# A hybrid decoder layer on one core: the running sum of the state-space decays and its three-way split are issued behind the first pair of stick-breaking heads

## The chip, the cores and the metric

The kernel runs on one core of a Trainium2 chip. The metric is the device time of one execution in microseconds (us); the time given for a kernel is the median of its runs.

## The reference, cut to what matters

The layer takes 1024 tokens behind 16 learned meta tokens (1040 positions), width 1024. One normalised input feeds three groups of heads, whose outputs are joined: stick-breaking attention (8 heads of 64), a state-space mixer (16 heads) and a latent attention (8 heads). A gated feed-forward stage follows. The change concerns the first two groups. Of the mixer it concerns the step sizes `dt`, and `Acs`, the running sum of the decays `dA` within a block of 128 positions, which the mixer's scan uses much later.

```python
dt = jax.nn.softplus(dt_raw.astype(F32) + dt_bias.astype(F32)) * valid[None, :, None].astype(F32)
a = -jnp.exp(a_log.astype(F32))
...
dA = (dt * a).reshape(b, nc, BLOCK, G, J)
Acs = jnp.cumsum(dA, axis=2)
...
seg = Acs[:, :, :, None] - Acs[:, :, None, :]
Ldec = jnp.exp(jnp.where(tri[None, None, :, :, None, None], seg, -jnp.inf))
...
z = jnp.einsum('bqhd,bkhd->bhqk', qb.astype(F32), kf) * scale
log_1m = jnp.where(mask, jax.nn.log_sigmoid(-z), 0.0)
between = lax.cumsum(log_1m, axis=3, reverse=True) - log_1m
w = jnp.exp(jnp.where(mask, jax.nn.log_sigmoid(z) + between, -jnp.inf))
return jnp.einsum('bhqk,bkhd->bqhd', w, vf)
...
h = h + jnp.concatenate([o_sb, o_ssm, o_mla], axis=-1) @ w_out[i].astype(dt)
```

## The kernel before, in words

All products are made of float32 operands split into a high and a low part, so a dense product is three matmuls per slice (lines 142 to 144 in `dense_fm`: high by high, low by high, high by low), accumulated in one of the two PSUM buffers of the pool `dpsum` (tile `d_ps`). One dense group for a chunk of positions is 24 matmuls. A buffer comes free when ScalarE (ACT) and VectorE (DVE) have copied its result out (`evac`).

The stretch that matters begins at about 80 us. The input has been normalised, keys and queries of the first pair of heads are ready (pair 0), and the program text gives, in this order: the value loads of pair 0, `step_sizes`, and then for each of four pairs `sb_attend`, the key and query products of the next pair, the next pair's values, and three of the twelve convolution units (`conv_unit`).

- `sb_attend` (line 676): for each of two heads and for j = 0 to 3, two rows of scores (`sb_row`) and one weighted sum (`weighted_values`). A row i covers 144 + 128 i keys: scores on TensorE (lines 661 to 665, tile `sc_ps`), a sigmoid on ACT (line 667) and a running product on DVE (line 669, tile `cm`, four buffers). The weighted sum transposes the rows on TensorE (lines 307 to 319, tiles `ptm` and `ptg`, pool `tp` with two buffers), splits them on ACT (302, 309) and DVE (303, 310), multiplies by the values (292 to 296, 311, tile `pv`, one buffer) and copies out (332 on ACT, 334 on DVE).
- The key copies of a pair (`k_evac`) are lines 591 and 592 on ACT and 593 and 594 on DVE, and those of the queries 600 and 601. The key tiles come from a ring `K` of four buffers.
- `conv_unit` (line 471): for each of three chunks a dense group, then ACT scales it into a tile of the ring `cacc` (479), three multiply-adds on DVE read the PSUM buffer (486), ACT takes a sigmoid into a tile of the ring `csig` (490), POOL multiplies (491) and a DMA stores. `cacc` and `csig` have two buffers each (pool `fl`), handed out in the order of the program text.
- `step_sizes` (line 410): a dense group of 96 columns, nine transposes into a `tp` buffer (`dtt`, 422), ACT's Abs and Exp (433, 434), then a softplus series on DVE (437 to 449), whose last result is the tile `d1`. Then comes what the change moves, lines 450 to 469: one matmul with a triangle of ones (`acum`, 451), its copy to `AT` (452), nine transposes (`acst`, 460), three copies on ACT (462) into `acs`, and eighteen DVE instructions that split `acs` into three bfloat16 parts of `A3` (463 to 469). `acs` lies in `raws[2]` and `raws[3]`, two of the four buffers of the ring `K`; `a2` (466) is a tile of the ring `csig`.

The order on each engine is not the program text's: a scheduler takes the instructions in the text's order of priority and places each on its engine's queue when, by its own plan, the operands and buffers are there. On the chip each engine then works through its queue in that order.

Of the kernel before, what the change touches and what calls it, by code (L numbers as in the profile page):

```python
# [11 lines left out]
F32 = mybir.dt.float32  # L12
# [12 lines left out]
T = SEQ + META  # L25
# [33 lines left out]
def tile_hybrid_block(ctx: ExitStack, tc: tile.TileContext, a: dict):  # L59
# [64 lines left out]
    def load_w(src, cols=1024, wp=None, make=None):  # L124
        wp = wp or wa
        raw = wp.tile([128, 1024], F32, tag="wraw", bufs=1, name="wraw")
        sp.dma_start(raw[:, :cols], src)
        hi = make("whi") if make else wp.tile([128, 1024], F32R, tag="whi", name="whi")
        act.copy(hi[:, :cols], raw[:, :cols])  # L129
        lo = make("wlo") if make else wp.tile([128, 1024], F32R, tag="wlo", name="wlo")  # L130
        pool.tensor_tensor(lo[:, :cols], raw[:, :cols], f32(hi[:, :cols]), op=ALU.subtract)  # L131
        return hi, lo

    def dense_fm(dpool, w, nkt, m, mov, chunks, evac):
        hi, lo = w
        for c0, n in chunks:
            ps = dpool.tile([128, 512], F32, tag="d", name="d_ps")
            for kt in range(nkt):
                mh, ml = mov(kt, c0, n)
                wh = hi[:, kt * m : (kt + 1) * m]  # L140
                wl = lo[:, kt * m : (kt + 1) * m]
                pe.matmul(ps[:m, :n], wh, mh, start=(kt == 0), stop=False)  # L142
                pe.matmul(ps[:m, :n], wl, mh, start=False, stop=False)  # L143
                pe.matmul(ps[:m, :n], wh, ml, start=False, stop=(kt == nkt - 1))  # L144
            with tc.high_priority(offset=1000):
                evac(ps, c0, n)
# [44 lines left out]
    def fill_tile(tag, name):  # L191
        return fl.tile([128, 388 if tag == "craw" else 384], F32, tag=tag, name=name)
# [13 lines left out]
    raws = [sbq.tile([128, 1024], F32, tag=tag, name="raw") for tag in ("KS", "KS", "K", "K")]  # L206
# [203 lines left out]
    def step_sizes():  # L410
        NC = 9 * 16
        pt = tp.tile([128, 512], F32, tag="tp", name="dtt")

        def dt_evac(ps, c0, n):
            dtx = fill_tile("cacc", "dtx")
            act.activation(dtx[:16, :n], ps[0:16, :n], AF.Identity, bias=dtb)
            krt = fill_tile("csig", "krt")
            act.copy(krt[:96, :n], ps[:96, :n])
            act.dma_start(s_kr[:, c0 : c0 + n], krt[32:96, :n])
            for b, (t0, w) in enumerate(BLOCKS):  # L420
                if c0 <= t0 < c0 + n:
                    pe.transpose(pt[:w, b * 16 : b * 16 + 16], dtx[:16, t0 - c0 : t0 - c0 + w], ident[:16, :16])

        dense_fm(dpool, load_w(a["w_dt"], KT * 96), KT, 96, hn_mov, CH_ALL, dt_evac)

        dx = fill_tile("cacc", "dx")[:, :NC]
        d1 = fill_tile("craw", "d1")[:, :NC]
        d2 = fill_tile("csig", "d2")[:, :NC]
        dve.memset(dx[:, 0:16], 0.0)
        dve.tensor_copy(dx[:META, 0:16], pt[:META, 0:16])  # L430
        dve.tensor_copy(dx[:, 16:NC], pt[:, 16:NC])
        dtv = DT.rearrange("p b h -> p (b h)")
        act.activation(d1, dx, AF.Abs)
        act.activation(d1, d1, AF.Exp, scale=-1.0)
        act.activation(acol, acol, AF.Exp)

        dve.tensor_scalar(d2, d1, 2.0, None, ALU.add)
        dve.reciprocal(d2, d2)
        dve.tensor_tensor(d1, d1, d2, op=ALU.mult)
        dve.tensor_tensor(d2, d1, d1, op=ALU.mult)  # L440
        dve.tensor_scalar(dtv, d2, 1.0 / 17, None, ALU.mult)
        for k in (15, 13, 11, 9, 7, 5, 3):
            dve.scalar_tensor_tensor(dtv, dtv, 1.0 / k, d2, ALU.add, ALU.mult)
        dve.scalar_tensor_tensor(dtv, dtv, 1.0, d1, ALU.add, ALU.mult)
        dve.tensor_scalar(dtv, dtv, 2.0, None, ALU.mult)
        dve.scalar_tensor_tensor(dtv, dx, 0.0, dtv, ALU.max, ALU.add)
        dve.tensor_scalar(acol, acol, -1.0, None, ALU.mult)
        d13 = d1.rearrange("p (b h) -> p b h", h=16)
        dve.tensor_tensor(d13, DT, acol.unsqueeze(1).to_broadcast([128, 9, 16]), op=ALU.mult)
        pt = tp.tile([128, 512], F32, tag="tp", name="acum")  # L450
        pe.matmul(pt[:, :NC], tri, d1, start=True, stop=True)
        dve.tensor_copy(AT.rearrange("p b h -> p (b h)"), pt[:, :NC])

        pool.memset(A3, 0.0)
        for i, (t0, n) in enumerate(CH_ALL):
            acs = (raws[2][:16, 0:272], raws[2][:16, 512:896], raws[3][:16, 0:384])[i]
            pt = tp.tile([128, 512], F32, tag="tp", name="acst")
            for b in range(3 * i, 3 * i + 3):
                b0, w = BLOCKS[b]
                pe.transpose(pt[:16, b0 - t0 : b0 - t0 + w], AT[:w, b, :], ident[:w, :w])  # L460
            c = slice(t0, t0 + n)
            act.copy(acs[:, :n], pt[:16, :n])
            dve.tensor_copy(A3[0:16, c], acs[:, :n])
            dve.tensor_tensor(acs[:, :n], acs[:, :n], A3[0:16, c], op=ALU.subtract)
            dve.tensor_copy(A3[32:48, c], acs[:, :n])
            a2 = fl.tile([16, 384], BF16, tag="csig", name="a2")
            dve.tensor_copy(a2[:, :n], acs[:, :n])
            dve.tensor_tensor(acs[:, :n], acs[:, :n], a2[:, :n], op=ALU.subtract)
            dve.tensor_copy(A3[64:80, c], acs[:, :n])
# [165 lines left out]
    for i, (q0, qn) in enumerate(((0, 256), (256, 384), (640, 384))):  # L635
# [3 lines left out]
        c0, n = CH_ALL[i]  # L639
# [8 lines left out]
    with ctx_sb as st:  # L648
        sbb = st.enter_context(tc.tile_pool(name="sbb", bufs=2, side="right", reuse_waits="tile"))
        sc = st.enter_context(tc.tile_pool(name="sc1", bufs=3, space=PSUM, reuse_waits="tile"))  # L650
        pvp = st.enter_context(tc.tile_pool(name="pv1", bufs=1, space=PSUM, reuse_waits="tile"))

        def sb_row(Qh, Kh, KSh, i):
            n_all = META + 128 * (i + 1)
            cm = sbb.tile([128, T], F32, tag="cm", bufs=4, name="cm")
            qs = Qh[:, 128 * i : 128 * (i + 1)]
            chunks = key_chunks(i)
            for c0, n in chunks[::-1]:
                ps = sc.tile([128, 512], F32, tag="sc", name="sc_ps")
                last = c0 + n >= n_all  # L660
                pe.matmul(ps[:, :n], qs, Kh[:, c0 : c0 + n], start=True, stop=False)
                pe.matmul(ps[:, :n], qs, KSh[:, c0 : c0 + n], start=False, stop=not last)
                if last:
                    m0 = n_all - 128 - c0
                    pe.matmul(ps[:, m0 : m0 + 128], identr, sb_mask, start=False, stop=True)
                    n = n_all - c0
                act.activation(cm[:, c0 : c0 + n], ps[:, :n], AF.Sigmoid, scale=-0.125)  # L667
            rev = cm[:, 0:n_all][:, ::-1]
            dve.tensor_tensor_scan(rev, rev, zcol.to_broadcast([128, n_all]), 1.0, ALU.mult, ALU.add)  # L669
            return cm  # L670

        pms = meta_tiles(sbb)

        def sb_attend(p, proj, values):
            Q, K, KS = proj
            for h in range(2):
                for j in range(NQ // 2):
                    rows = [sb_row(Q[h], K[h], KS[h], 2 * j + e) for e in range(2)]  # L680
                    weighted_values(tp, pvp, sbb, j, rows, values[0], h, [x[p, 64 * h : 64 * (h + 1)] for x in (s_osbh, s_osbl)], pms[j % 2], values[1])

        values = load_value_steps(sbv, sbb, 0)
        step_sizes()
        convs = [8, 9, 10, 11, 0, 1, 2, 3, 4, 5, 6, 7]
        for p in range(4):
            sb_attend(p, proj, values)
            if p < 3:
                if p == 1:
                    sb_values(1, [load_w(a["w_sbv"][1, u]) for u in range(2)], range(9))  # L690
                proj, k_evac, q_evac = sb_project(p + 1)
                dense_fm(dpool, load_w(a["w_sbk"][p + 1]), KT, 128, hn_mov, CH_ALL, k_evac)
                dense_fm(dpool, load_w(a["w_sbq"][p + 1]), KT, 128, hn_real, CH_REAL, q_evac)
                values = load_value_steps(sbv, sbb, p + 1)
            for u in convs[3 * p : 3 * p + 3]:
                conv_unit(u)
# [1023 lines left out]
```

## Time and profile before

| | |
|---|---|
| median of 3 runs | 1817.64 us (1814.70 to 1820.21) |
| profiled execution | 1819.26 us |
| its span, first to last instruction | 1817.3 us |
| TensorE (PE) busy, matmuls | 1722.8 us, 95% |
| VectorE (DVE) busy | 1214.3 us, 67% |
| ScalarE (ACT) busy | 860.0 us, 47% |
| GpSimd (POOL) busy | 858.4 us, 47% |
| mean granted TensorE clock | 0.972 of full |

A busy share is a mean over the whole span; what bounds a stretch is read from the stretches. The granted clock has two levels, 2.4 GHz (1.00) and 1.2 GHz (0.50); a figure between them is a mean over a stretch that saw both, and time in which TensorE does nothing counts in the figure as well.

### The profile page before, as it was taken

To read this page: it belongs to the slowest core of one execution; us is meant where nothing else is said; L and a number is where in the kernel's file an instruction comes from. 1 tells how busy PE (TensorE), PEld (TensorE's weight loads), DVE (VectorE), ACT (ScalarE), POOL (GpSimd) and SP (SyncE) were. 2 spreads that over 40 slices of the span, in tenths; PEclk is the share of its full clock that TensorE was granted. 3 is DMA by queue.
4 is the path that set the end of the run, shared out by engine and by line. 5 is a ranking of instruction groups with operands and counts; after the bars stand their busy time and mean duration, and the time that the engine had idled before them with its cause. 6 is when DMAs were issued, how large, how long until landed. Compare 5 with 4: busy or idle time off the path is not lost.

```text
span 1817.3 us, 26447 instructions
## 1 busy us (share of the span) xinstructions
PE 1722.8 (95%) x9769; PEld 1506.0 (83%) x9769; DVE 1214.3 (67%) x1801; ACT 860.0 (47%) x1878; POOL 858.4 (47%) x597
## 2 busy tenths in 40 slices
PE   7969999999999999999999998999999999799997
PEld 7859998999987778998888876778888888677787
DVE  8686655777544673455576558967776667899854
ACT  7545564555566646775544424422232223334333
POOL 4433334343366557563321345634333234678783
PEclk9969999999998999999999998999999999899999
DMA  4211232222443546347221342232222233733102
GB/s 157 60 53 44 78 88 73 64 70 66 116 148 106 187 159 171 103 124 263 78 88 53 108 140 102 64 99 83 80 76 81 71 98 140 286 100 95 47 1 93
DMA packets 121012, 186.93 MB, mean 103 GB/s; under 512 B 21986, under 2 KB 81412, under 8 KB 120884
## 3 DMA queue, kind: packets, MB, share of 16 engines
q1 hardware_dynamic: 101488, 169.69, 29.6%
q10 hardware_dynamic: 19396, 15.56, 2.8%
q8 instruction: 77, 1.26, 0.3%
q14 instruction: 51, 0.42, 0.1%
HBM read 131.61 MB, written 53.60 MB: 102 GB/s over the span
## 4 chain that ended last, share of the span: by engine, by line
PE 68%; DVE 17%; ACT 4%; issue 3%; DMA 3%; POOL 3%; SPq 1%; ACTq 0%; DVEq 0%; POOLq 0%
PE d_ps L142 8%; PE d_ps L143 8%; PE d_ps L144 8%; PE b_ps L1295 7%; PE b_ps L1297 7%; PE b_ps L1296 7%; DVE raw L1081 2%; PE ptg L317 2%; PE b_ps L1498 1%; PE b_ps L1497 1%; PE ptg L319 1%; PE pv L295 1%; PE b_ps L1496 1%; PE pv L296 1%; DVE hF L1084 1%
## 5 line engine op out<-in xcount | busy, mean ns | idle before, releaser
L142 PE MATMUL d_ps<-hnh,whi 128*128 128x384 f32 (+6 forms) x744 | 247.3, 333 | 1.4 <-DVE go L534 0.7
L144 PE MATMUL d_ps<-hnl,whi 128*128 128x384 f32 (+6 forms) x744 | 246.7, 332 | 0.0
L143 PE MATMUL d_ps<-hnh,wlo 128*128 128x384 f32 (+6 forms) x744 | 245.6, 330 | 0.0
L131 POOL TENSOR_TENSOR wlo<-wraw,whi 128x1024 fp32r<-128x1024 f32 (+1 forms) x57 | 135.9, 2385 | 212.0 <-ACT whi L129 203.1
L1078 POOL TENSOR_TENSOR op<-raw,op 128x512 fp32r<-128x512 f32 x83 | 125.2, 1534 | 42.1 <-ACT op L1077 38.9
L142 PEld LDWEIGHTS d_ps<-hnh,whi 128*128 128x128 f32 (+1 forms) x744 | 140.4, 189 | 5.5 <-DVE go L534 1.3
L144 PEld LDWEIGHTS d_ps<-hnl,whi 128*128 128x128 f32 (+1 forms) x744 | 140.6, 189 | 3.3 <-issue 1.0
L143 PEld LDWEIGHTS d_ps<-hnh,wlo 128*128 128x128 f32 (+1 forms) x744 | 140.4, 189 | 2.3 <-issue 0.2
L1295 PE MATMUL b_ps<-T,wh 128*128 128x512 f32 x352 | 138.4, 393 | 0.9 <-DVE u L1084 0.9
L1296 PE MATMUL b_ps<-T,wl 128*128 128x512 f32 x352 | 138.1, 392 | 0.0
L1297 PE MATMUL b_ps<-T,wh 128*128 128x512 f32 x352 | 138.0, 392 | 0.0
L303 DVE TENSOR_TENSOR pl<-ptg,ph 128x512 fp32r<-128x512 f32 (+1 forms) x160 | 99.6, 628 | 46.3 <-ACT ph L302 44.7
L1078 POOL TENSOR_TENSOR wlo<-raw,whi 128x1024 fp32r<-128x1024 f32 (+1 forms) x22 | 52.7, 2395 | 152.9 <-ACT whi L1077 152.9
L669 DVE TENSOR_TENSOR_SCAN cm<-cm,zcol 128x144 f32<-128x144 f32 (+3 forms) x64 | 103.9, 1634 | 17.8 <-ACT cm L667 17.4
L1077 ACT CAST op<-raw 128x512 fp32r<-128x512 f32 x107 | 61.4, 618 | 96.7 <-PE d_ps L1498 49.4
L302 ACT CAST ph<-ptg 128x512 fp32r<-128x512 f32 (+1 forms) x160 | 85.3, 541 | 36.3 <-PE ptg L319 24.7
L1078 POOL TENSOR_TENSOR wl<-raw,wh 128x512 fp32r<-128x512 f32 x46 | 69.8, 1526 | 58.8 <-ACT wh L1077 58.0
L1084 DVE TENSOR_TENSOR hF<-hF,b_ps 128x512 f32<-128x512 f32 (+1 forms) x96 | 59.2, 635 | 46.4 <-PE b_ps L1562 23.9
L486 DVE SCALAR_TENSOR_TENSOR cacc<-d_ps,cw,cacc 128x384 f32<-128x384 f32 (+3 forms) x108 | 61.8, 572 | 38.2 <-ACT cacc L479 36.2
L1077 ACT CAST wh<-raw 128x512 fp32r<-128x512 f32 x88 | 52.9, 616 | 67.0 <-PE b_ps L1297 64.0
L129 ACT CAST whi<-wraw 128x1024 fp32r<-128x1024 f32 (+1 forms) x57 | 58.9, 1033 | 49.4 <-PE d_ps L144 23.4
L1496 PE MATMUL b_ps<-op 128*128 128x512 f32 x183 | 72.8, 401 | 9.9 <-DVE hF L1084 6.2
(452 smaller groups left out, 5352.8 us busy)
## 6 DMA issues: line engine op xcount, KB each, us to landing
raw<-in_w_gate_dram SPq DMA_DIRECT2D x22, 512.0 KB
raw<-in_w_up_dram SPq DMA_DIRECT2D x22, 512.0 KB, 4.1
s_hid<-gs SPq DMA_DIRECT2D x44, 256.0 KB, 2.4
raw<-in_w_down_dram SPq DMA_DIRECT2D x22, 512.0 KB, 5.2
raw<-s_hid SPq DMA_DIRECT2D x22, 512.0 KB, 4.3
wraw<-in_w_o_dram SPq DMA_DIRECT2D x16, 512.0 KB, 4.0
wraw<-in_w_xbc_dram SPq DMA_DIRECT2D x12, 512.0 KB, 3.8
s_xs<-csig SPq DMA_DIRECT2D x24, 192.0 KB, 2.6
```

Source lines behind the costliest of these rows:

```text
L131: pool.tensor_tensor(lo[:, :cols], raw[:, :cols], f32(hi[:, :cols]), op=ALU.subtract)
L142: pe.matmul(ps[:m, :n], wh, mh, start=(kt == 0), stop=False)
L143: pe.matmul(ps[:m, :n], wl, mh, start=False, stop=False)
L144: pe.matmul(ps[:m, :n], wh, ml, start=False, stop=(kt == nkt - 1))
L303: dve.tensor_tensor(pl[:, :n], pt[:, :n], f32(ph[:, :n]), op=ALU.subtract)
L669: dve.tensor_tensor_scan(rev, rev, zcol.to_broadcast([128, n_all]), 1.0, ALU.mult, ALU.add)
L1077: act.copy(hi, value)
L1078: eng.tensor_tensor(lo, value, f32(hi), op=ALU.subtract)
L1295: pe.matmul(banks[j], hi[:, ks], UH[u][k], start=start and k == 0, stop=False, skip_group_check=skip)
L1296: pe.matmul(banks[j], lo[:, ks], UH[u][k], start=False, stop=False, skip_group_check=skip)
L1297: pe.matmul(banks[j], hi[:, ks], UL[u][k], start=False, stop=stop and k == 3, skip_group_check=skip)
L1496: pe.matmul(banks[o], wh[:, os], hh, start=first, stop=False, skip_group_check=not start)
```

## The change

`step_sizes` ends with `d1` and returns it; what followed becomes `decay_sums`, which is called behind `sb_attend` of pair 0. `acs` no longer lies in the ring `K` but in a tile of the ring `cm` that the call takes. `a2` stays in the ring `csig`, `d1` in the ring `craw`. No instruction is added or taken away: one matmul, nine transposes, three ACT copies, nineteen DVE instructions and one memset (on POOL, at the start of the program in both). Nothing of it issues a DMA.

```diff
--- before.py
+++ after.py
@@ -447,13 +447,18 @@
         dve.tensor_scalar(acol, acol, -1.0, None, ALU.mult)
         d13 = d1.rearrange("p (b h) -> p b h", h=16)
         dve.tensor_tensor(d13, DT, acol.unsqueeze(1).to_broadcast([128, 9, 16]), op=ALU.mult)
+        return d1
+
+    def decay_sums(d1, space):
+
+        NC = 9 * 16
         pt = tp.tile([128, 512], F32, tag="tp", name="acum")
         pe.matmul(pt[:, :NC], tri, d1, start=True, stop=True)
         dve.tensor_copy(AT.rearrange("p b h -> p (b h)"), pt[:, :NC])
 
         pool.memset(A3, 0.0)
         for i, (t0, n) in enumerate(CH_ALL):
-            acs = (raws[2][:16, 0:272], raws[2][:16, 512:896], raws[3][:16, 0:384])[i]
+            acs = space[:16, t0 : t0 + n]
             pt = tp.tile([128, 512], F32, tag="tp", name="acst")
             for b in range(3 * i, 3 * i + 3):
                 b0, w = BLOCKS[b]
@@ -681,10 +686,12 @@
                     weighted_values(tp, pvp, sbb, j, rows, values[0], h, [x[p, 64 * h : 64 * (h + 1)] for x in (s_osbh, s_osbl)], pms[j % 2], values[1])
 
         values = load_value_steps(sbv, sbb, 0)
-        step_sizes()
+        steps = step_sizes()
         convs = [8, 9, 10, 11, 0, 1, 2, 3, 4, 5, 6, 7]
         for p in range(4):
             sb_attend(p, proj, values)
+            if p == 0:
+                decay_sums(steps, sbb.tile([128, T], F32, tag="cm", bufs=4, name="acs"))
             if p < 3:
                 if p == 1:
                     sb_values(1, [load_w(a["w_sbv"][1, u]) for u in range(2)], range(9))
```

The scheduler places almost everything between 92 and 272 us anew; the queues of all engines agree again from about TensorE's 1,575th matmul on (272 us), but for some neighbours that change places much later. Line numbers of the changed kernel are five higher from line 450 on, and seven from `sb_attend`'s calls on (661 is 666, 669 is 674, 486 is 491, 593 is 598).

TensorE where the second chunk of pair 1's keys ends (`d_ps<-hnh` and `hnl` are dense matmuls). Before:

```order
L144 MATMUL d_ps<-hnl_143,whi 128x384
L142 MATMUL d_ps<-hnh_136,whi 128x384
L143 MATMUL d_ps<-hnh_136,wlo 128x384
L144 MATMUL d_ps<-hnl_144,whi 128x384
L451 MATMUL acum<-d_1028,tri 128x144
L460 MATMUL acst<-identr,AT 16x16
L460 MATMUL acst<-identr,AT 16x128 x8
L307 MATMUL ptm<-identr,cm 16x128
L308 MATMUL ptm<-identr,cm 16x128
L317 MATMUL ptg<-identr,cm 128x128
```

and now:

```order
L142 MATMUL d_ps<-hnh_136,whi 128x384
L143 MATMUL d_ps<-hnh_136,wlo 128x384
L144 MATMUL d_ps<-hnl_144,whi 128x384
L666 MATMUL sc_ps<-K,Q 128x400
L667 MATMUL sc_ps<-KS,Q 128x400
L311 MATMUL pv<-pm,V 128x256
L307 MATMUL ptm<-identr,cm 16x128
L308 MATMUL ptm<-identr,cm 16x128
L295 MATMUL pv<-ph,V 128x128
L142 MATMUL d_ps<-hnh_129,whi 128x384
L143 MATMUL d_ps<-hnh_129,wlo 128x384
L144 MATMUL d_ps<-hnl_137,whi 128x384
```

The running sum no longer follows the second chunk; weighted sums of head 0 and the third chunk's matmuls (`hnh_129` again, lines 142 to 144) do.

VectorE at the end of the split. Before (`K` and `KS` are the keys' copies, `A` and `a` the bfloat16 parts):

```order
L468 TENSOR_TENSOR raw<-raw,a_1089 16x384
L469 CAST A_121<-raw 16x384
L334 TENSOR_TENSOR oT<-pv,half 64x2x128
L469 CAST A_121<-raw 16x384
L303 TENSOR_TENSOR pl<-ptg,ph 128x512
L669 SCALAR_TENSOR_TENSOR cm<-cm,zcol 128x912
L303 TENSOR_TENSOR pl<-ptg,ph 128x384
L593 TENSOR_TENSOR K<-d_ps,K 64x272
L594 TENSOR_TENSOR KS<-d_ps,K 64x272
```

and now, at the split's beginning:

```order
L303 TENSOR_TENSOR pl<-ptg,ph 128x384
L457 COPY AT<-acum 128x144
L334 TENSOR_TENSOR oT<-pv,half 64x2x128
L468 CAST A_121<-acs 16x272
L674 SCALAR_TENSOR_TENSOR cm<-cm,zcol 128x144
L469 TENSOR_TENSOR acs<-acs,A_121 16x272
L674 SCALAR_TENSOR_TENSOR cm<-cm,zcol 128x272
L674 SCALAR_TENSOR_TENSOR cm<-cm,zcol 128x400
L470 CAST A_121<-acs 16x272
L472 CAST a_1622<-acs 16x272
L468 CAST A_121<-acs 16x384 x2
L473 TENSOR_TENSOR acs<-acs,a_1622 16x272
```

The keys' copies of pair 1 no longer stand behind the split; the split stands behind the last weighted sum of pair 0 (`pl`), among the running products of pair 1 (`cm`).

TensorE in the second head of pair 0, now: where the first chunk of convolution unit 9 ends,

```order
L317 MATMUL ptg<-identr,cm 128x128
L143 MATMUL d_ps<-hnh_136,wlo 128x272
L144 MATMUL d_ps<-hnl_144,whi 128x272
L311 MATMUL pv<-pm,V 128x256
L295 MATMUL pv<-ph,V 128x256
L666 MATMUL sc_ps<-K,Q 128x384
L667 MATMUL sc_ps<-KS,Q 128x384
L670 MATMUL sc_ps<-sb_mask,identr 128x128
```

and where the next dense matmul stands, 165 matmuls and transposes later, among them the moved ones:

```order
L667 MATMUL sc_ps<-KS,Q 128x272
L670 MATMUL sc_ps<-sb_mask,identr 128x128
L666 MATMUL sc_ps<-K,Q 128x400
L667 MATMUL sc_ps<-KS,Q 128x400
L670 MATMUL sc_ps<-sb_mask,identr 128x128
L142 MATMUL d_ps<-hnh_129,whi 128x388
L143 MATMUL d_ps<-hnh_129,wlo 128x388
L144 MATMUL d_ps<-hnl_137,whi 128x388
```

In these 165 no dense matmul stands; the second chunk of unit 9 begins behind them. In the queue of before, dense matmuls and the attention's change places all through pair 0's second head.

## Rows read from the trace of the kernel before

**Rows 1.** By stretch: us; PE, PEld, DVE, ACT, POOL busy (count); granted clock, DMA, GB/s
```profile
90.00:100.00 10.00, 5.75 (x31) 5.06 (x31) 7.10 (x8) 6.31 (x12) 4.98 (x4) 0.95 0.33 107
100.00:110.00 10.00, 5.11 (x20) 3.13 (x19) 7.36 (x18) 1.23 (x4) 3.35 (x5) 0.67 0.19 54
110.00:120.00 10.00, 7.51 (x26) 5.32 (x24) 9.72 (x17) 4.39 (x12) 3.61 (x3) 0.50 0.18 53
120.00:130.00 10.00, 7.14 (x31) 6.39 (x31) 9.72 (x15) 7.16 (x19) 1.97 (x2) 0.51 0.01 2
130.00:140.00 10.00, 7.61 (x39) 7.13 (x39) 5.92 (x9) 2.71 (x7) 0.72 (x1) 0.83 0.11 26
150.00:200.00 50.00, 50.00 (x352) 48.77 (x351) 36.36 (x57) 29.89 (x69) 20.28 (x15) 1.00 0.20 60
```

**Rows 2.** Who waited for whom, PE alone, 85 to 140 us: total, times, longest
```profile
PE sc_ps L661 <- ACT cm L667: 4.5, 3, 3.8
PE acum L451 <- DVE d L449: 4.5, 1, 4.5
PE ptg L317 <- DVE pm L310: 4.3, 2, 2.4
```

**Rows 3.** Timeline, ACT about 97 us: start, length, instruction, [idle before <- releaser]
```profile
97.29 1.28 ACT L667 ACT_TABLE_LOAD   x1
```

**Rows 4.** Timeline, PE, DVE and ACT from 101 to 134 us, in order of time
```profile
101.67 0.52 PE L144 MATMUL d_ps<-hnl,whi 128*128 128x384 f32 x1
...
123.92 0.35 DVE L469 CAST A<-raw 16x384 bf16<-16x384 f32 x1
124.89 0.39 ACT L591 CAST K<-d_ps 64x272 fp32r<-64x272 f32 x1
124.92 2.05 DVE L669 TENSOR_TENSOR_SCAN cm<-cm,zcol 128x912 f32<-128x912 f32 x1
...
133.58 0.69 PE L142 MATMUL d_ps<-hnh,whi 128*128 128x384 f32 x1 [0.43 <-DVE KS L594]
```

**Rows 5.** DVE's groups on the page: count | busy us, mean ns | idle before
```profile
L303 DVE TENSOR_TENSOR pl<-ptg,ph 128x512 fp32r<-128x512 f32 (+1 forms) x160 | 99.6, 628 | 46.3 <-ACT ph L302 44.7
L669 DVE TENSOR_TENSOR_SCAN cm<-cm,zcol 128x144 f32<-128x144 f32 (+3 forms) x64 | 103.9, 1634 | 17.8 <-ACT cm L667 17.4
L486 DVE SCALAR_TENSOR_TENSOR cacc<-d_ps,cw,cacc 128x384 f32<-128x384 f32 (+3 forms) x108 | 61.8, 572 | 38.2 <-ACT cacc L479 36.2
```

**Rows 6.** DVE's groups by shape, 137 to 420 us
```profile
L669 DVE TENSOR_TENSOR_SCAN cm<-cm,zcol 128x912 f32<-128x912 f32 x6 | 14.7, 2445 | 1.2 <-ACT cm L667 1.2
L669 DVE TENSOR_TENSOR_SCAN cm<-cm,zcol 128x784 f32<-128x784 f32 x6 | 12.2, 2041 | 3.6 <-ACT cm L667 3.6
L310 DVE TENSOR_TENSOR pm<-ptm,pm 16x256 fp32r<-16x256 f32 x23 | 9.5, 414 | 5.2 <-ACT pm L309 4.4
L334 DVE TENSOR_TENSOR oT<-pv,half 64x256 f32<-64x256 f32 x23 | 9.4, 411 | 9.0 <-ACT half L332 8.3 <-PE sc_ps L662 0.3
```

**Rows 7.** Instructions on tile raw alone, 107 to 125 us, columns as in the first group
```profile
107.00:125.00 18.00, 0.00 (x0) 0.00 (x0) 9.79 (x18) 1.31 (x3) 0.00 (x0) 0.50 0.10 30
```

**Rows 8.** DVE's groups by line, 107 to 125 us: the split's first subtraction
```profile
L464 DVE TENSOR_TENSOR raw<-raw,A 16x384 f32<-16x384 f32 (+1 forms) x3 | 4.0, 1345 | 0.0
```

**Rows 9.** Timeline, DVE and POOL about 110 us
```profile
109.41 1.88 DVE L464 TENSOR_TENSOR raw<-raw,A 16x272 f32<-16x272 f32 x1
109.75 1.25 POOL L405 TENSOR_TENSOR vst<-vsp,vst 128x512 f32<-128x512 f32 x1
112.41 0.54 DVE L464 TENSOR_TENSOR raw<-raw,A 16x384 f32<-16x384 f32 x1
```

**Rows 10.** Timeline of PE from 292 us: behind a gap, then slow and fast
```profile
292.56 0.28 PE L307 MATMUL ptm<-identr,cm 128*16 128x128 f32 x1 [1.97 <-DVE cm L669]
295.81 0.53 PE L144 MATMUL d_ps<-hnl,whi 128*128 128x388 f32 x1
297.24 0.34 PE L143 MATMUL d_ps<-hnh,wlo 128*128 128x388 f32 x1
```

## The prediction

> **What bounds the kernel now.** I read the busy times by stretch first, then TensorE's waits and the timeline of the one stretch where TensorE is not full, and last VectorE's groups, which give the prices.
>
> From 150 to 200 us TensorE is busy for 50.00 of 50 us at the full clock, with 352 matmuls [rows 1], so one costs 50/352 = 0.142 us there. From 90 to 140 us it is not full: 5.75, 5.11, 7.51, 7.14 and 7.61 us of each 10, which leaves 16.9 us idle; and the granted clock falls to 0.50. Busy time times the clock's missing share (5.75 x 0.05 + 5.11 x 0.33 + 7.51 x 0.50 + 7.14 x 0.49 + 7.61 x 0.17) is another 10.5 us. So the stretch loses 27.4 us against a full TensorE at 2.4 GHz.
>
> The waits say for what: 4.5 us for ACT's sigmoids, 4.5 us for `d1`, 4.3 us for the copies of `pm` [rows 2]. The timeline says why nothing else filled the time: the second chunk of pair 1's keys is done at 101.67 us, the next dense matmul starts at 133.58 us [rows 4]. Both PSUM buffers of the dense groups are full in between, since the keys can only be copied into ring `K` once the split has left its two tiles: the last split instruction (line 469) runs at 123.92 us, the first copy of keys (line 591) at 124.89 us [rows 4]. VectorE, meanwhile, is busy for 9.72 of 10 us [rows 1].
>
> **What is removed.** The split leaves ring `K` and moves behind pair 0, so the keys' copies need not wait for it. All 27.4 us of that stretch are up for gain.
>
> **What stays there.** The softplus series stays, and so does the wait before it. Between Abs and the next sigmoid ACT loads its tables, of which the second load takes 1.28 us from 97.29 us on [rows 3], and TensorE's longest wait, 3.8 us, hangs on that [rows 2]. In the new queue ACT also makes two copies of keys before this load. I leave 4.5 us for this, the total of that row. Behind it VectorE now works through the series, the running products of head 0 and three chunks of keys' copies, while TensorE has dense work again. It comes before them to the third key chunk, to the second weighted sum and to the first query chunk. Walking the new queues with the rows' durations I get holds of 1.0, 1.7 and 1.4 us there and some 2 us of smaller ones: 6.1 us, an estimate. Together 10.6 us; between 4.5 (VectorE always in time) and 16.9 (as much idle time as before).
>
> **What is added.** The moved instructions cost what they cost before; their place costs something. `a2` lies in ring `csig`, which hands its two buffers out in the order of the program text, and there the split now stands ahead of convolution units 8 to 10 and behind all of pair 0. No unit can take its sigmoid before the split has used `a2`. Two chunks fit into `cacc`, two more into the PSUM buffers; then the dense work stops. The new queue shows it: behind the first chunk of unit 9, 165 matmuls and transposes of the attention and the split, and no dense one. A full TensorE needs 165 x 0.142 = 23.4 us for them. The dense group behind them waits until VectorE's three multiply-adds have emptied the buffer with unit 8's third chunk, and in its new queue VectorE has all this to do, from the running product of row 5 of head 1 up to the last of the three:
>
> - ten running products: the eight lengths once, 8 x 1.634 us [rows 5], and 784 and 912 columns a second time, 2.04 + 2.45 us [rows 6]: 17.6 us
> - eleven `pl` at 0.628 us: 6.9 us; four `pm` at 0.414 and five `oT` at 0.411 us: 3.7 us [rows 5, 6]
> - the split: 9.79 us for its 18 instructions [rows 7], and about 0.3 us for the copy to `AT`: 10.1 us
> - these three multiply-adds and one of unit 9 at 0.572 us [rows 5]: 2.3 us
>
> That is 40.6 us, 17.2 us more than TensorE needs. VectorE's load rather than its latency is the price, and the nearest row says it is real: with the split and the attention alone before it VectorE was busy for 9.72 of 10 us while TensorE stood at 7.1 to 7.5 us at half clock [rows 1]. From below: with the subtraction of line 464 at its shortest and every running product at the 2.05 us against 2.45 us of [rows 4, 6], 35.3 us, or 11.9 us lost. From above: 4 us more where VectorE itself waits for the end of a weighted sum, 21 us lost.
>
> A rule bears on one item. Line 464 took 1.88 us for 272 columns beside a POOL subtraction of 1.25 us, and 0.54 us for 384 columns without one [rows 9]; all three took 4.0 us [rows 8]. The Trainium skill (SBUF — State Buffer, "Who interferes with whom") says that a VectorE instruction with two SBUF inputs and a GpSimd instruction that reads SBUF exclude each other, and the later one blocks. By that rule the subtractions would cost 3 x 0.54 = 1.6 us where POOL is quiet, and the sum would be 2.4 us lower. In the new queue POOL has little beside the split, so I keep that for the lower end; it is not in the sum.
>
> **The clock.** After a gap of 1.97 us at 292.56 us TensorE's dense matmuls last 0.53 us, and 0.34 us again from 297 us on [rows 10]: some 3.5 us at 1.2 GHz, a loss of about 1.7 us for one such gap. I take 1.7 us for the gap that stays near 98 us and 3 us for the stretch of 165, where TensorE waits anyway half the time: 4.7 us, between 0 and 12.
>
> **The sum.** 10.6 + 17.2 + 4.7 - 27.4 = +5.1 us. Behind the stretch both queues hold the same work, and dense matmuls are plentiful, so I cost the rest at nothing: pair 1's attention and nine dense chunks hide it, and VectorE has done more of its share by then than before. Against the profiled execution (1819.26 us) this gives 1824.4 us; the median of the runs lies 1.6 us lower, so I predict 1817.64 + 5.1 = **1822.7 us**. Its own range, 1816 to 1830, comes from the bounds above with most of them near the middle.
>
> **The rivals.**
>
> 1. *VectorE is quicker than the sum, and the change pays.* The stretch takes 35.3 us (-5.3), the holds near 100 us shrink to 4.5 (-6.1), the second clock term goes (-3): +5.1 - 14.4 = -9.3 us, 1808.3 us. For it: POOL is quiet there, and the running products are longer than 2.05 us only beside POOL. Against it: VectorE also has to wait for ACT and TensorE in a chain of short steps. It decides where the 165 take less than about 32 us.
> 2. *The clock stays low in the stretch.* In the profile TensorE at 7.1 us of 10 under a loaded VectorE ran at 0.50 [rows 1]. At 1.2 GHz the 165 need up to 2 x 23.4 = 46.8 us, more than VectorE's 40.6: 6.2 us more, and some 2 us for the steps between. +13.3 us, 1830.9 us. The Trainium skill (TensorE: Matmul & The Clock Gate, "What's actually happening") says that the slow clock is the default and activity releases it. By that rule this rival comes true if half-empty counts as idle; [rows 1] bear it out only where gaps of over 2 us stood beside the busy time.
> 3. *It makes no difference.* From about 272 us on both queues are the same; a transfer or a buffer that sets the time later would swallow what comes before. Against it: TensorE is full there, so an earlier or later start carries through. Near 1817.6 us.
>
> **How the numbers follow.** A measurement of this kernel can tell 0.3% (5.5 us) from no change. The forecast gets 0.55: it lies on that edge, so 0.28 slower, 0.25 same, 0.02 faster. Rival 1 gets 0.17 (0.13 faster, 0.04 same), rival 2 0.18 (0.16 slower, 0.02 same), rival 3 0.10 (same). Together faster 0.15, same 0.41, slower 0.44. The range runs from rival 1's time, 1808.5, to a little over rival 2's, 1833, and leaves out an upper end where all bounds meet.
>
> **What would show it.** Right: near 100 us pair 1's keys are copied at once and the third key chunk starts some 30 us earlier than 133.58; the last dense matmul before a hole and the next one lie 38 to 45 us apart, with VectorE over 90% busy and the split inside; from there on TensorE is full. Wrong: the hole is under 32 us, or dense matmuls stand in it, or TensorE is still empty for over 15 us before the hole; then the first term or the second is mis-sized. If the hole's matmuls last twice as long throughout, rival 2 is right.

## The result, and the profile of the changed kernel

| | before | changed |
|---|---|---|
| median of 6 runs each | 1819.41 us (1814.70 to 1823.91) | 1826.41 us (1824.56 to 1828.06) |
| profiled execution, its span | 1819.26 us, 1817.3 us | 1824.56 us, 1822.6 us |
| mean granted clock | 0.972 | 0.976 |

The ratio is 1.0037, with a 95% interval from 1.0022 to 1.0051: the change costs about 7 us (5.3 us between the two spans). That is slower by a little more than the 0.3% that the prediction takes as the least that can be told from no change.

The stretches that answer to [rows 1], TensorE's busy time first, the granted clock third from the end. First 90 to 140 us of the changed kernel, then the place of the hole:

```profile
90.00:100.00 10.00, 6.98 (x34) 6.00 (x33) 6.46 (x9) 6.62 (x12) 5.39 (x4) 0.83 0.42 116
100.00:110.00 10.00, 9.61 (x57) 9.07 (x57) 9.28 (x17) 6.14 (x17) 3.45 (x4) 1.00 0.20 57
110.00:120.00 10.00, 6.98 (x23) 5.36 (x23) 9.76 (x13) 6.21 (x14) 5.38 (x5) 0.66 0.23 66
120.00:130.00 10.00, 9.86 (x55) 8.16 (x54) 9.80 (x13) 5.86 (x13) 3.04 (x3) 1.00 0.17 52
130.00:140.00 10.00, 10.00 (x74) 9.51 (x73) 6.21 (x12) 5.76 (x13) 3.39 (x3) 1.00 0.16 35
...
160.00:170.00 10.00, 7.14 (x53) 5.71 (x51) 7.50 (x12) 5.13 (x12) 1.44 (x2) 1.00 0.05 13
170.00:180.00 10.00, 7.83 (x51) 5.78 (x50) 7.78 (x18) 6.07 (x17) 1.67 (x3) 1.00 0.12 29
180.00:190.00 10.00, 6.34 (x29) 4.95 (x29) 9.68 (x17) 5.56 (x14) 2.18 (x3) 0.71 0.07 20
190.00:200.00 10.00, 6.48 (x35) 5.95 (x35) 9.90 (x11) 3.94 (x10) 4.35 (x3) 0.84 0.11 33
200.00:210.00 10.00, 10.00 (x66) 9.98 (x65) 5.38 (x11) 4.94 (x10) 2.03 (x4) 0.94 0.18 59
```

From 90 to 140 us 6.6 us are idle (16.9 before), and the slow clock takes 6.98 x 0.17 + 6.98 x 0.34 = 3.6 us (10.5 before): 10.1 us lost instead of 27.4. In exchange TensorE is 30% empty from 160 to 200 us (12.2 us idle), where [rows 1] show it full.

The timeline of the changed kernel, TensorE: the first matmul of the third key chunk, the last dense matmul ahead of the hole and the first one behind it:

```profile
103.48 0.44 PE L142 MATMUL d_ps<-hnh,whi 128*128 128x384 f32 x1 [0.20 <-DVE KS L599]
...
157.09 0.29 PE L144 MATMUL d_ps<-hnl,whi 128*128 128x272 f32 x1
...
196.42 0.44 PE L142 MATMUL d_ps<-hnh,whi 128*128 128x388 f32 x1 [2.33 <-DVE cacc L491]
```

The third key chunk starts at 103.48 us, 30.1 us earlier than in [rows 4]. The hole is 39.3 us long, from start to start. Its cause stands in the timelines of VectorE and ACT: the last two reads of `a2` (line 473) and the first sigmoid of a convolution unit (495), which takes the buffer of the earlier of the two:

```profile
185.24 0.55 DVE L473 TENSOR_TENSOR acs<-acs,a 16x384 f32<-16x384 f32 x1
186.64 0.54 DVE L473 TENSOR_TENSOR acs<-acs,a 16x384 f32<-16x384 f32 x1
...
186.50 0.43 ACT L495 ACTIVATE csig<-cacc 128x272 f32<-128x272 f32 x1
```

To follow where time goes behind the stretch, two marks serve, both on TensorE: mark 1, the first matmul `d_ps<-ones,grow` (line 153), behind the four pairs' attention, and mark 2, the first transpose `invt` (line 997), in the latent attention. The timeline of the kernel before:

```profile
498.59 0.40 PE L153 MATMUL d_ps<-ones,grow 128*16 128x1 f32 x3
...
739.41 0.27 PE L997 MATMUL invt<-identr,inv 128*8 128x128 f32 x1
```

and of the changed one:

```profile
502.47 0.40 PE L153 MATMUL d_ps<-ones,grow 128*16 128x1 f32 x3
...
744.67 0.27 PE L1004 MATMUL invt<-identr,inv 128*8 128x128 f32 x1
```

So 3.9 us are lost by mark 1 and 1.4 us more by mark 2; at the end of the span it is 5.3 us again.

### The profile page after: what moved, and what is told of

Read it like the earlier page. It is cut to its first block, busy times and chain, and to the rows that moved or that the text cites. A ratio compares the mean times of both kernels' runs of the same rounds, so it can differ in the third digit from the quotient of the medians.

```text
span 1822.6 us, 26444 instructions
## 1 busy us (share of the span) xinstructions
PE 1724.1 (95%) x9769; PEld 1506.2 (83%) x9769; DVE 1216.7 (67%) x1801; ACT 859.8 (47%) x1878; POOL 858.3 (47%) x597
## 4 chain that ended last, share of the span: by engine, by line
PE 70%; DVE 17%; ACT 5%; issue 3%; DMA 2%; POOL 2%; SPq 1%; ACTq 0%; DVEq 0%; POOLq 0%
PE d_ps L142 8%; PE d_ps L143 8%; PE d_ps L144 8%; PE b_ps L1302 7%; PE b_ps L1304 7%; PE b_ps L1303 7%; DVE raw L1088 2%; PE ptg L317 2%; PE pv L296 1%; PE pv L295 1%; PE ptg L319 1%; PE b_ps L1505 1%; PE b_ps L1504 1%; PE b_ps L1503 1%; DVE hF L1091 1%
```

## The experiments

Theory A is that of the prediction: the ring `K` costs the kernel before 27 us, and `a2` in the ring `csig` makes a hole of 20 us. Theory B: VectorE's load is what costs time, wherever the tiles lie. Theory C: the stretch does not set the time at all. Differences in this table are to the kernel before (498.59, 739.41, 1817.3 us), read from the same two rows of each trace and from the spans, one profiled execution each; the ratios are of runs on the same chip.

| kernel | mark 1 | mark 2 | span | ratio, 95% interval |
|---|---|---|---|---|
| changed | +3.9 | +5.3 | +5.3 | 1.0037 (1.0022 to 1.0051) |
| r_after, the same again | +1.4 | +5.5 | +7.3 | 1.0036 (1.0024 to 1.0047) |
| r_before, before again | +0.1 | -0.8 | -0.5 | |
| e2, `acs` in `cm`, split in its place | -20.9 | -20.7 | -23.4 | 0.9903 (0.9887 to 0.9918) |
| e1, `a2` in `craw` | -14.0 | -10.6 | -9.7 | 0.9972 (0.9959 to 0.9984) |
| e3, call behind the units | -16.7 | -8.5 | -9.5 | 0.9951 (0.9938 to 0.9964) |
| e7, both of these | -20.3 | -15.7 | -16.8 | 0.9928 (0.9908 to 0.9948) |
| e4, no sums, no split | -20.5 | -18.2 | -17.9 | 0.9917 (0.9904 to 0.9930) |
| e5, split cut short | -2.8 | -2.9 | -4.4 | 0.9991 (0.9981 to 1.0000) |
| e11, `acs` in `craw`, call as changed | -2.2 | -2.3 | -5.1 | 0.9991 (0.9978 to 1.0004) |
| e9, `acs` in `craw`, split in its place | -13.1 | -9.4 | -6.3 | 0.9989 (0.9973 to 1.0005) |

**The first half of the change alone (e2).**

```diff
--- before
-    def step_sizes():
+    def step_sizes(space):
...
-            acs = (raws[2][:16, 0:272], raws[2][:16, 512:896], raws[3][:16, 0:384])[i]
+            acs = space[:16, t0 : t0 + n]
...
-        step_sizes()
+        step_sizes(sbb.tile([128, T], F32, tag="cm", bufs=4, name="acs"))
```

> The kernel before with one edit: acs takes a tile of the ring cm, so that the ring K is free for pair 1's keys; running sum and split stay where they are. Theory A (before loses 27.4 us from 90 to 140 us because the keys' copies wait for the split in ring K): the third key chunk starts near 103 to 110 us instead of 133.58, idle time and slow clock in 90 to 140 us fall from 27.4 us to about 10 (the wait for the softplus) plus some 5 for VectorE's split: 1805 to 1812 us, ratio 0.992 to 0.996. Theory B (VectorE, 9.72 of 10 us busy there, is the bound, and the ring only hides it): TensorE gains under 5 us, 1814 to 1819 us, ratio 0.997 to 1.000. Theory C: no change, 1.000.

Measured: 1800.65 us against 1817.24, better than theory A asked; B and C are out for this half. The scheduler plans the queues anew for every edit, so this, like each run below, is the edit and its new order together. By stretch, e2:

```profile
90.00:100.00 10.00, 7.44 (x34) 7.15 (x33) 7.95 (x17) 4.65 (x12) 5.33 (x4) 0.83 0.39 107
100.00:110.00 10.00, 10.00 (x49) 8.50 (x48) 6.13 (x14) 5.32 (x11) 6.67 (x7) 1.00 0.38 99
110.00:120.00 10.00, 9.18 (x58) 7.38 (x56) 3.95 (x7) 5.32 (x10) 2.81 (x3) 1.00 0.18 63
120.00:130.00 10.00, 4.93 (x17) 4.70 (x18) 9.73 (x17) 2.65 (x8) 2.18 (x1) 0.67 0.16 52
130.00:140.00 10.00, 10.00 (x64) 9.72 (x63) 9.80 (x16) 6.19 (x14) 3.88 (x3) 0.99 0.10 29
```

TensorE runs through the chunks of keys and queries at full clock while VectorE works off the series and has room left (6.13 and 3.95 of 10 us). The split then falls at 115 to 135 us, and it still costs something there: of TensorE's two longest waits from 85 to 140 us, the first ends at 125.62 us, within the split, and the second at 96.03 us, ahead of it. e2:

```profile
PE d_ps L142 <- DVE Q L601: 5.0, 1, 5.0
PE d_ps L142 <- DVE KS L594: 2.6, 1, 2.6
```

So the whole gain lay in the first half of the change, and moving the split threw it away. This kernel beats both.

**`a2` out of the ring `csig` (e1).**

```diff
--- changed
-            a2 = fl.tile([16, 384], BF16, tag="csig", name="a2")
+            a2 = fl.tile([16, 384], BF16, tag="craw", name="a2")
```

> The changed kernel with one edit: a2 takes a tile of the ring craw, which nothing else asks for between the step sizes and the latent heads, and no longer one of csig. Theory A (a2 in csig makes the hole): TensorE's queue has no stretch of 165 without dense matmuls before unit 10 ends; the 39.3 us between the last dense matmul of unit 9's first chunk and the next one shrink to under 8 us; the 20 us lost there come back for the most part, so the time is 1805 to 1812 us, ratio to the kernel before 0.992 to 0.996. Theory B (VectorE's load makes the hole, wherever a2 lies): VectorE has the same 40 us of work there, its queue still holds up the buffers of the dense groups, at least 10 us stay lost: 1816 to 1823 us, ratio 0.998 to 1.002. Theory C (the stretch does not set the time; what was measured comes from behind 300 us): as the changed kernel, 1.002 to 1.005.

Measured: 1813.07 us, ratio 0.9972, between the ranges of A and B. The hole is gone: from 150 to 190 us TensorE is busy for 10.00 of each 10 us. By stretch, e1:

```profile
180.00:190.00 10.00, 10.00 (x71) 9.32 (x70) 5.35 (x10) 5.08 (x12) 2.44 (x4) 1.00 0.09 34
190.00:200.00 10.00, 7.69 (x59) 7.11 (x58) 9.85 (x19) 4.19 (x14) 5.66 (x3) 0.91 0.32 104
```

By mark 1 it is 17.9 us ahead of the changed kernel (484.60 against 502.47), close to the 17.2 + 3 us of the prediction. But the split is not free: from 190 to 200 us VectorE is full (9.85), and TensorE stands at 7.69. And 3.4 of 14.0 us are lost again between the marks, of which below.

**The call behind the units (e3), and with `a2` in `craw` as well (e7).** The edit of e3; e7 adds that of e1:

```diff
--- changed
-            if p == 0:
-                decay_sums(steps, sbb.tile([128, T], F32, tag="cm", bufs=4, name="acs"))
...
             for u in convs[3 * p : 3 * p + 3]:
                 conv_unit(u)
+            if p == 0:
+                decay_sums(steps, sbb.tile([128, T], F32, tag="cm", bufs=4, name="acs"))
```

> The changed kernel with one edit: running sum and split are called behind the three convolution units that follow pair 0, not ahead of them; a2 stays in csig. Theory A (what counts is that a2 stands ahead of the units in csig's order): the units take their sigmoids without waiting for the split, the hole is gone, 1805 to 1812 us as with a2 in craw, ratio 0.992 to 0.996; but unit 11 and on now wait for the split in csig, which costs nothing, as the split is done before pair 1's keys. Theory B: a hole of the same size only lies later, 1818 to 1826. Theory C: 1.002 to 1.005.

> The changed kernel with both edits: a2 in craw, and the call behind the three convolution units of pair 0. Its queue from the scan's beginning has nearly the order of the run with the call behind the units. Theory A with order: ahead by 17 to 20 us at 560 us, and 6 to 9 us of it lost between 585 and 680 us as in that run; ratio 0.994 to 0.997. Rival (a2 in csig behind the units still cost something there): at 560 us further ahead than that run by 3 us or more; ratio below 0.993.

Measured: 1809.34 and 1803.76 us. e3 is where A put it: what made the hole was that `a2` stood ahead of the units in the order of `csig`. e7 came out a little faster than A said, and by mark 1 it is 3.6 us ahead of e3. That speaks for the rival, by which `a2` in `csig` costs something behind the units, too, where A had called it nothing. It is not shown: the two ratios' intervals overlap, that of e7 reaches into A's range, and two profiles of the changed kernel lie 2.5 us apart at mark 1.

**Without the sums and the split (e4).**

> The changed kernel without running sum and split: this leaves out the decays' sums altogether (AT and A3 are set to zero once), so the output is not the reference's. It is the least that any place for them can give. Theory A: the hole is gone and with it 10 us of VectorE's work that has room beside TensorE: 1803 to 1810 us, and no more than 4 us below the kernel with a2 in craw. Theory B: VectorE's 10 us are on the path, so it lies 10 us or more below the kernel with a2 in craw. Theory C: 1.000 to 1.004.

Measured: 1801.33 us, below the range of A. By mark 1 it is 6.5 us ahead of e1, by mark 2 7.6 us, and 11.7 us by the medians. A had said at most 4, B 10 or more: at e1's place most of the split's VectorE time comes on top, so B is right in part. At its old place (e2) it costs nothing net: e2 and e4 are level at mark 1 (477.71 and 478.13 us).

**The hole's length: a shorter split (e5), and `acs` out of `cm` (e11).** In e5 the lines 469, 470, 473 and 474 are taken out; e11 is

```diff
--- changed
-            acs = space[:16, t0 : t0 + n]
+            acs = fill_tile("craw", "acs")[:16, :n]
...
-                decay_sums(steps, sbb.tile([128, T], F32, tag="cm", bufs=4, name="acs"))
+                decay_sums(steps, None)
```

> The changed kernel, split cut short: for each chunk VectorE makes only the first part of A3 and the copy a2; both subtractions and the two lower parts are left out (12 of 18 instructions, 6.3 us by their rows in the changed kernel's trace), so the output is not the reference's. a2 still stands in csig ahead of the convolution units. In the new queues the hole in TensorE's dense work holds 139 matmuls and transposes instead of 165. Theory A (VectorE's queue makes the hole's length): between the two dense matmuls VectorE has 6.3 us of split, one running product of 912 columns and two pl less, so 39.3 us become 28 to 31, and the time falls by 5 to 8 us against the changed kernel: ratio to the kernel before 0.999 to 1.001. Theory B (the hole is as long as a chain of short steps through ACT, VectorE and TensorE makes it, and VectorE's load is not what counts): it shrinks by the 26 matmuls alone, to 35 us or more, and the time falls by less than 3 us: ratio 1.002 or more.

> The changed kernel with acs in the ring craw, one tile for each chunk, instead of a tile of cm; a2 stays in csig. It asks whether one of the four cm buffers, held for the length of the split, lengthens the hole. Theory A (a2 in csig makes the hole, VectorE's load its length): the hole stays, at 143 matmuls instead of 165, and 33 to 39 us; the time is at most 5 us below the changed kernel, ratio 0.999 to 1.003. Rival (the cm buffer is what the running products wait for): the hole shrinks by 10 us or more, ratio 0.995 to 0.998.

Measured: 1816.29 and 1815.70 us. e5's timeline at the two ends of the hole:

```profile
156.06 0.29 PE L144 MATMUL d_ps<-hnl,whi 128*128 128x272 f32 x1
...
184.74 0.44 PE L142 MATMUL d_ps<-hnh,whi 128*128 128x388 f32 x1
```

That is 28.7 us instead of 39.3: some 10 us of VectorE's work fewer (6.3 of split, the rest running product and `pl`), 10.6 us shorter. VectorE's load makes the length, in this pair one for one, as A said. In e11 the hole lies from 156.50 to 189.68 us, 33.2 us with 143 matmuls: the `cm` buffer is not what makes it. But the time missed A's bound: 1815.70 us is 9.2 us below the changed kernel on the same chip (1824.92, r_after), where A allowed 5. The hole is 6.1 us shorter, with one running product and two `pl` fewer in it; whether that comes from the free `cm` buffer or from the new order stays open.

**`acs` in `craw`, split in its place (e9).** The edit is the first line of e11's, made to the kernel before.

> The kernel before with acs in the ring craw, one tile for each chunk, split left in its place: like the run with acs in cm, the ring K is free, but behind 300 us TensorE's queue has the order of the run with a2 in craw and of the run without the split, not that of the kernel before. Theory A with order (freeing K gives 20 us or more by 300 us, and that order then loses 6 to 7 us in the scan near 640 us, where TensorE waits some 4 us for VectorE's y at the line of yo): ahead of the kernel before by 18 to 24 us at 560 us and by 12 to 17 us at 720 us; ratio 0.991 to 0.995. Rival (those losses near 640 us were chance or the split's): no such wait, ratio 0.988 to 0.991.

Measured: ratio 0.9989, a miss for both: by mark 1 it is only 13.1 us ahead. Two waits of 4.3 us stand between 90 and 140 us: for a sigmoid (line 667), which the kernel before has with 3.8 us and e2 does not, and a new one for ACT's copy into `acs` (462). That a ring of two buffers makes that copy late was not tried by itself. The part on the order held, though: TensorE's wait for `y` is there with 4.2 us.

**Twice the same (r_after, r_before).**

> The changed kernel again, for a second profile. In the first one it was 3.3 us behind the kernel before at 300 us of the span, and 3 us more were lost in two steps, 1.5 us near 700 us and 1.4 us near 845 us, where the queues of the two kernels differ for some 60 and some 170 places of TensorE's order. Theory A (these two steps come from the re-planned order): both come again, 1.2 to 1.8 us each. Rival (they are chance): steps elsewhere or none. The ratio to the kernel before is 1.002 to 1.005 as measured.

> The kernel before again, one look, for a second profile: how far two executions of the same queues drift apart from place to place. Theory A: no step over 0.7 us near 700 and 845 us. Rival: steps of 1 to 2 us come anywhere in it by chance, so that what was read as the order's effect is not.

The ratio came again (1.0036), and so did the hole: 157.25 to 196.59 us, 39.3 us. Of the two small steps behind it, the one near 845 us came again with 1.5 us, as theory A said, the one near 700 us with 0.9 instead of 1.5. The granted clock, third from the end, goes with it; 700 to 715 us in before, r_before, changed and r_after:

```profile
700.00:715.00 15.00, 13.01 (x79) 12.01 (x80) 7.55 (x20) 12.01 (x33) 11.95 (x9) 0.89 0.59 155
700.00:715.00 15.00, 13.30 (x81) 12.54 (x81) 7.63 (x20) 11.36 (x30) 11.93 (x10) 0.89 0.56 155
700.00:715.00 15.00, 12.80 (x79) 11.84 (x78) 6.67 (x18) 11.76 (x32) 12.32 (x9) 0.77 0.68 182
700.00:715.00 15.00, 13.10 (x80) 12.14 (x79) 7.04 (x18) 11.92 (x32) 12.72 (x10) 0.77 0.71 190
```

It is lower already ahead of the first matmul that has another place in the changed kernel's queue (at 708.69 us in the queue of before). The same matmul in before and in changed, at 2.4 and at 1.2 GHz:

```profile
706.72 0.34 PE L961 MATMUL sc_ps<-mlo,mhi 96*128 96x400 f32 x1
...
711.18 0.54 PE L968 MATMUL sc_ps<-mlo,mhi 96*128 96x400 f32 x1
```

So TensorE's new order is not what the step begins with, and theory A's reason for it is not borne out. From 840 to 860 us the clock is 0.91, 1.00, 0.83 and 0.83 in the same four. Between the marks r_after fared otherwise than the first profile. It was 1.4 us late at mark 1 and 5.5 at mark 2, and most of these 4.1 us were lost near 500 us, at a wait of 1.3 us for a DMA (`xs<-s_xs`) that the first profile did not have and at a slow clock behind it (r_after):

```profile
500.00:510.00 10.00, 8.71 (x49) 8.04 (x49) 3.87 (x6) 4.63 (x8) 6.09 (x4) 0.66 0.95 259
```

The first profile has 10.00 us busy and 1.00 there. And r_before gained 0.9 us between the marks on the queues of before, with steps of up to 1.6 us both ways. One profile's step of 1 or 2 us is therefore no evidence, and the theory's part on r_before fell.

**The order behind the stretch.** Between the marks e1, e9 and e4 lose 3.4, 3.7 and 2.3 us, e3 and e7 8.2 and 4.6 us. Since r_after lost 4.1 us with nearly the order of before, only e3's 8.2 us stand out by their size; for e1, e9 and e4 the evidence is that the order and a wait go together. In those five the scheduler gave TensorE another order through the mixer's scan. e5 and e11 keep the order of before there row by row, e2 but for some neighbours at its beginning, and all three lose nothing (0.2 us at most). The wait of TensorE for `y` from 560 to 720 us, before:

```profile
PE yo L796 <- DVE y L806: 1.4, 1, 1.4
```

and e1:

```profile
PE yo L803 <- DVE y L813: 4.8, 2, 4.1
```

e9, which has e1's order there, and e4, which nearly has it, show that wait with 4.2 us each; e2 has 0.6. e3 and e7 have 0.6 and 0.8, so what costs their 8.2 and 4.6 us is something else in their order, which was not followed up.

## Why the prediction was right, and where its steps were not

The time came within 4 us of the forecast (1826.41 against 1822.7), by the mechanism that it named; that it came so near is in part luck, since errors in the sum cancelled. Step by step:

- **What is removed: right.** e2 changes nothing in the text but the ring of `acs` and is 20.9 us ahead at mark 1. By its rows above it still loses 8.5 us idle and 3.0 us of clock from 90 to 140 us, most of it at its waits of 2.6 and 5.0 us: 11.4 us instead of 27.4. The other 5 us of its gain lie outside this stretch.
- **What stays near 100 us: the size right, its parts not.** 10.6 us and 1.7 us of clock were predicted, 10.1 us with the clock were measured. But the wait for the sigmoid, put at 4.5 us, is 1.1 us; in its place VectorE is late more often than thought. TensorE's waits from 85 to 140 us, which answer to [rows 2]:

```profile
PE ptg L317 <- DVE pm L310: 2.4, 1, 2.4
PE ptm L307 <- DVE cm L674: 2.1, 1, 2.1
PE sc_ps L666 <- ACT cm L672: 1.1, 2, 0.6
PE d_ps L142 <- DVE KS L599: 0.8, 2, 0.6
```

- **The hole: cause and place right; its length right by two errors that cancelled.** 39.3 us against 40.6. VectorE by line from 156 to 196.2 us, the work that the prediction counted (count, busy us, mean ns, idle before):

```profile
L674 DVE TENSOR_TENSOR_SCAN cm<-cm,zcol 128x784 f32<-128x784 f32 (+7 forms) x10 | 15.4, 1552 | 0.6 <-ACT cm L672 0.5
L303 DVE TENSOR_TENSOR pl<-ptg,ph 128x512 fp32r<-128x512 f32 (+1 forms) x11 | 6.6, 621 | 2.5 <-ACT ph L302 2.3
...
L474 DVE CAST A<-acs 16x384 bf16<-16x384 f32 (+1 forms) x3 | 1.9, 648 | 0.1
...
L473 DVE TENSOR_TENSOR acs<-acs,a 16x384 f32<-16x384 f32 (+1 forms) x3 | 1.5, 501 | 0.0
L469 DVE TENSOR_TENSOR acs<-acs,A 16x384 f32<-16x384 f32 (+1 forms) x3 | 1.5, 496 | 0.0
L470 DVE CAST A<-acs 16x384 bf16<-16x384 f32 (+1 forms) x3 | 1.3, 448 | 0.1
L472 DVE CAST a<-acs 16x384 bf16<-16x384 f32 (+1 forms) x3 | 1.0, 329 | 0.1
L468 DVE CAST A<-acs 16x384 bf16<-16x384 f32 (+1 forms) x3 | 0.9, 324 | 0.0
```

  `pl` (6.9 us predicted) came nearly as counted. The ten running products took 15.4 us instead of 17.6: 1.634 us was a mean over the whole kernel. The split's 18 instructions took 8.1 us instead of 9.8, since its first subtraction, line 469, took 1.5 us, not the 4.0 of [rows 8]. The Trainium skill (SBUF — State Buffer, "Who interferes with whom") had it right with its exclusion of VectorE and GpSimd: POOL was quiet here, the prediction's 1.6 us by that rule was the better price, and the 4.0 us were those of another neighbourhood. So the work was put some 4 us too high. On the other side VectorE is busy for only 11.33 + 22.38 = 33.7 us of the hole (rows below) and idle for 5.6, which the sum had at nothing and only the upper bound, with 4 us, allowed for.
- **What the hole costs: near the 17.2 + 3 us, by a price that was wrong.** 0.142 us for a matmul is a mean over a stretch with dense ones. In the next stretch of the changed kernel without matmuls of lines 142 to 144, from 223.00 to 263.89 us, TensorE is nearly full and does 339 in 40.9 us, 0.121 us each. By that price the 165 need 19.9 us, and 39.3 - 19.9 = 19.4 us are lost, clock included. Counted as the other two terms are, as idle time and slow clock, it is 12.2 + 3.5 = 15.7 us from 160 to 210 us.
- **VectorE over 90% busy: only in the second half.** Of the hole's two parts,

```profile
157.09:173.00 15.91, 12.61 (x91) 10.36 (x89) 11.33 (x16) 9.01 (x22) 2.56 (x4) 1.00 0.18 54
173.00:196.42 23.42, 14.52 (x79) 11.17 (x78) 22.38 (x38) 13.83 (x37) 4.49 (x6) 0.85 0.09 26
```

  VectorE is busy for 96% of the second, with the split, and for 71% of the first, where it waits for ACT's `ph` and TensorE for its `pl`: that is the upper bound's case, "VectorE itself waits", in part.
- **The rivals.** The first asked for a hole under 32 us: it is 39.3. The second fell for the most part: at 7.1 and 7.8 us busy of 10 the granted clock was 1.00. Only behind 180 us it was lower, 0.71, 0.84 and 0.94, which cost 3.5 us; the sum had 3. The third fell with e1, e2 and e3.
- **"I cost the rest at nothing": not borne out.** The measured terms of the stretch add up to 10.1 + 19.4 - 27.4 = +2.1 us, or -1.6 with the hole at 15.7; the two profiles have +3.9 and +1.4 at mark 1. So the 5.1 us were probably too many for the stretch, and the medians say 6.6 to 7.0 us for the whole. By mark 2 both profiles stand at +5.3 and +5.5. Of r_after's 4.1 us between the marks most belongs to one late DMA and the clock behind it. Of the 1.4 us of the first profile the larger part is lost near 707 us, at a lower clock that both profiles of the changed kernel have there (0.77 against 0.89). The two orders do differ for some neighbours, which was known beforehand and priced at nothing, but only from just behind this place on; what lowers the clock stays open, and r_before drifts by 0.9 us on its own.

## What to carry to other kernels

When a change frees a buffer and moves work as well, price the two halves apart: here the buffer alone gives 1%, and the move, past the users of a second ring that is handed out in program order, costs more than that. Look for every ring that a moved step draws from, and ask whose turn it takes. Where a scheduler plans the queues, an edit early on can give a late stage another order that costs several us, and two profiles of one kernel differ by 1 to 3 us from place to place; compare the queues to the end, and take a second profile, before pricing the rest.

## What was not expected of the hardware

A half-empty TensorE kept its clock for 20 us. At 7.14 and 7.83 us of 10 busy it was granted 1.00. In this profile it fell behind two gaps, one of 2.33 us at the hole's end (196.42 us, above) and one of 2.40 us, here with a transpose before and behind it:

```profile
182.59 0.27 PE L319 MATMUL ptg<-identr,cm 128*128 128x128 f32 x1
185.26 0.47 PE L317 MATMUL ptg<-identr,cm 128*128 128x128 f32 x1 [2.40 <-DVE pm L310]
```

But the gap is not a condition. In r_after, with the same queues and the same 7.14 and 7.81 us busy at 1.00 from 160 to 180 us, the transposes are slow ahead of that gap already, and no gap from 165 us up to there is over 0.9 us:

```profile
183.30 0.42 PE L319 MATMUL ptg<-identr,cm 128*128 128x128 f32 x1
185.42 0.47 PE L317 MATMUL ptg<-identr,cm 128*128 128x128 f32 x1 [1.70 <-DVE pm L310]
```

And VectorE is held by POOL in instructions with one input, too. In e2, the cast of 272 columns into `a2` (line 467) begins behind POOL's subtraction (131) and ends 0.15 us behind it:

```profile
119.77 2.41 POOL L131 TENSOR_TENSOR wlo<-wraw,whi 128x1024 fp32r<-128x1024 f32 x1 [3.15 <-ACT whi L129]
120.01 2.32 DVE L467 CAST a<-acs 16x272 bf16<-16x272 f32 x1
```

The same cast took 0.29 us in the changed kernel, where POOL was quiet. In e2 all but its first 0.65 us lie within the 5.0 us that TensorE waits for the queries' copies. The Trainium skill (SBUF — State Buffer, "Who interferes with whom") names casts among the instructions that can take the shared ports; the trace agrees, and the prediction had weighed the rule for the subtractions alone.
